# Remainders of the weights on GpSimd instead of VectorE, in a two-layer hybrid trunk

## The chip, the cores and the metric

The kernel runs on one core of a Trainium2 chip. The time is what the device takes for one execution, in microseconds. TensorE is called PE below (PEld its weight loads), VectorE DVE, ScalarE ACT, GpSimd POOL, and SyncE SP; these are the names in the profile.

## The reference, cut to what matters

Two layers over 512 tokens of width 1024, float32. Layer 0 mixes by attention: 8 heads of forgetting attention (softmax with a cumulative decay) and 8 stick-breaking heads, head size 64. Layer 1 mixes by a gated short convolution. Each mixer is followed by a gated MLP of width 2816 with a causal convolution of width 3.

```python
h = x
for layer in range(DEPTH):
    i = layer // 2
    if layer % 2 == 0:
        h = h + attention_mixer(h, ...)      # proj = rms_norm(h) @ w_in ; 16 heads ; o @ w_out
    else:
        h = h + short_conv_mixer(h, ...)     # gate_b * conv3(gate_c * u) @ w_out
    h = h + conv_ffn(h, ...)                 # u = conv3(rms_norm(h) @ w_up); (silu(g) * val) @ w_down
```

## The kernel before, in words

Every product with a weight matrix is made of three passes of PE in a reduced format, so that the result keeps nearly float32's precision: a number a is written as hi + lo, where hi is a rounded to the format (float32r) and lo is the remainder a - hi; the product is hi x hi + hi x lo + lo x hi (`mm3`, and `mm3_rhs` where the weights are the moving operand). The activations are split in this way where they arise; the weights are split when they are loaded.

**The weights' pipeline.** The program writes down all 198 pieces of weights in the order of their use (`want`); a piece ("chunk") is up to 128 x 1056 numbers, mostly 128 x 1024. `weights()` hands out the next chunk and before that calls `load` for as many as keep two in advance. For one chunk, `load` issues the DMA into `raw` (by SP, L223), then the main copy `whi` on ACT (L226), then, through `rest`, the remainder `wlo` = raw - whi (L233). `raw`, `whi` and `wlo` have three buffers each: a new main copy waits until PE has done its last matmul with the main copy of three chunks ago, and the DMA of a chunk waits until the remainder of three chunks before has read its buffer.

**The stages.** First come the transposes of x and the first norm. Then attention, up to about 310 us: the projections run as `columns`, tokens on the partitions ("token-major"), two chunks for each of queries (L490 to L492, kind 0), keys and values of four groups of four heads. `heads` takes the sums of squares (L521, L523), the reciprocal root (`rsqrt`, ten small DVE steps, L316 to L328) and scales (L532, L535); `turn_heads` transposes and splits (L549 to L554). `logits` makes the scores of a pair of heads for half of the tokens (L571 to L577); for forgetting heads softmax follows (L588 to L595), for stick-breaking ones two sigmoids, a scan (L604) and a product (L605). `turn` transposes the weights of attention (L623) and splits them into `pt` (L625, L628); POOL fills a part of each `pt` with zeros (L633). `weigh` multiplies by the values (L647, L648) and adds up (L657, L658); `output` applies the output projection to a group (L248 to L250). The projections of later groups are generators that are run in small bits between these steps (`fill`). After that come the MLP's up-projection (44 chunks), its down-projection (24), the short convolution, and the second MLP, whose down-projection runs with the weights as the moving operand again.

The order in the program is an order of wishes: a scheduler that works with its own estimates of each instruction's cost puts the final order on every engine, and each engine then works strictly in that order.

Of the kernel before, what the change touches and what calls it, by code (L numbers as in the profile page):

```python
# [22 lines left out]
ALU = mybir.AluOpType  # L23
# [25 lines left out]
def trunk(  # L49
# [7 lines left out]
    act, dve, pe, pool = nc.scalar, nc.vector, nc.tensor, nc.gpsimd  # L57
# [13 lines left out]
    def f32(ap):  # L71
        return ap.bitcast(F32)
# [89 lines left out]
    def behind(later, earlier):  # L162

        tc.add_manual_dep(
            later.ins, earlier.ins.name,
            mybir.DependencyInfo(mybir.DependencyClass.NoSync, mybir.DependencyReason.DATA), reason="order",
        )
# [11 lines left out]
    def after(us, fn):  # L179
        later.append((clock[0] + us, len(later), fn))  # L180
        later.sort(key=lambda e: e[0])
# [31 lines left out]
    def load(i, last=None):  # L213
        dram, k0, nk, parts = wanted[i]
        n = sum(parts[1::2])
        raw = wp.tile([P, CHUNK], F32, tag="raw", name=f"raw{i}")
        hi = wp.tile([P, CHUNK], F32R, tag="whi", name=f"whi{i}", bufs=3)
        lo = wp.tile([P, CHUNK], F32R, tag="wlo", name=f"wlo{i}", bufs=3)
        v = raw[:, 0:nk * n].rearrange("p (k c) -> p k c", c=n)
        to = 0  # L220
        for c0, width in zip(parts[::2], parts[1::2]):
            with nc.allow_non_contiguous_dma(reason="eight columns"):
                nc.sync.dma_start(  # L223
                    v[:, :, to:to + width], dram[k0 * P:(k0 + nk) * P, c0:c0 + width].rearrange("(k p) c -> p k c", p=P))
            to += width
        made = act.activation(hi[:, 0:nk * n], raw[:, 0:nk * n], AF.Copy)  # L226
        if last is not None:
            behind(made, last)

        def rest():  # L230
            if i in unsplit:
                unsplit.remove(i)
                dve.tensor_tensor(lo[:, 0:nk * n], raw[:, 0:nk * n], f32(hi[:, 0:nk * n]), op=ALU.subtract)  # L233
        unsplit.add(i)
        after(LATER, rest)
        return rest, [t[:, 0:nk * n].rearrange("p (k c) -> p k c", c=n) for t in (hi, lo)]
# [682 lines left out]
```

## Time and profile before

| | us |
|---|---|
| median of 3 runs | 1243.5 (1242.23 to 1245.99) |
| the profiled execution | 1243.43, of which span 1241.7 |
| busy in the span: PE, DVE | 1207.4, 765.5 |
| busy in the span: ACT, POOL | 500.3, 21.2 |

A row of the timeline reads: start, duration (us), engine, line, operation, tile written <- tiles read, shape, count, and in brackets how long the engine had stood idle before it and who released it. Tile names stand without their buffer numbers. Rows on waits read: engine, line, who released it, microseconds in total, times, longest.

### The profile page before, as it was taken

To read this page: it belongs to the slowest core of one execution; us is meant where nothing else is said; L and a number is where in the kernel's file an instruction comes from. 1 tells how busy PE (TensorE), PEld (TensorE's weight loads), DVE (VectorE), ACT (ScalarE), POOL (GpSimd) and SP (SyncE) were. 2 spreads that over 40 slices of the span, in tenths; PEclk is the share of its full clock that TensorE was granted. 3 is DMA by queue.
4 is the path that set the end of the run, shared out by engine and by line. 5 is a ranking of instruction groups with operands and counts; after the bars stand their busy time and mean duration, and the time that the engine had idled before them with its cause. 6 is when DMAs were issued, how large, how long until landed. Compare 5 with 4: busy or idle time off the path is not lost.

```text
span 1241.7 us, 15526 instructions
## 1 busy us (share of the span) xinstructions
PE 1207.4 (97%) x6129; PEld 1002.8 (81%) x6129; DVE 765.5 (62%) x1248; ACT 500.3 (40%) x814; POOL 21.2 (2%) x101
## 2 busy tenths in 40 slices
PE   8999999898999999999999999999999999999998
PEld 7988988776888888888888888888888888888886
DVE  6687778787767777773333555555777676762212
ACT  6465665555444434342222222233444344442120
POOL 3000000000000000000000000000000000000000
PEclk9999999999999999999999999999999999999999
DMA  5312212111233333323333333333233323232330
GB/s 175 104 45 59 57 46 69 34 52 51 86 102 89 98 97 90 102 81 93 94 94 98 102 87 100 89 98 100 88 94 93 102 86 102 87 100 85 109 112 34
DMA packets 175273, 108.16 MB, mean 87 GB/s; under 512 B 4604, under 2 KB 168492, under 8 KB 175200
## 3 DMA queue, kind: packets, MB, share of 16 engines
q1 hardware_dynamic: 174944, 107.01, 29.0%
q8 instruction: 48, 0.79, 0.3%
q0 software_dynamic: 256, 0.16, 0.1%
q14 instruction: 25, 0.20, 0.1%
HBM read 105.06 MB, written 2.10 MB: 86 GB/s over the span
## 4 chain that ended last, share of the span: by engine, by line
PE 88%; DVE 7%; ACT 3%; issue 1%; DMA 1%; SPq 0%; DVEq 0%; ACTq 0%
PE psb L248 11%; PE psb L250 11%; PE psb L249 11%; PE psa L248 11%; PE psa L249 11%; PE psa L250 11%; PE psa L490 4%; PE psa L492 4%; PE psa L491 4%; PE psb L492 2%; PE psb L491 2%; PE psb L490 2%; DVE rest L604 1%; PE psc L623 1%; ACT whi L226 1%; DVE wlo L233 1%
## 5 line engine op out<-in xcount | busy, mean ns | idle before, releaser
L226 ACT ACTIVATE whi<-raw 128x1024 fp32r<-128x1024 f32 (+2 forms) x198 | 208.3, 1053 | 360.2 <-PE psb L249 130.9
L233 DVE TENSOR_TENSOR wlo<-raw,whi 128x1024 fp32r<-128x1024 f32 (+2 forms) x198 | 240.3, 1214 | 169.5 <-ACT whi L226 168.6
L248 PE MATMUL psb<-hs_hi,whi 128*128 128x512 f32 x480 | 189.9, 396 | 0.0
L250 PE MATMUL psb<-hs_hi,wlo 128*128 128x512 f32 x480 | 189.9, 396 | 0.0
L249 PE MATMUL psb<-hs_lo,whi 128*128 128x512 f32 x480 | 188.8, 393 | 0.0
L248 PE MATMUL psa<-hs_hi,whi 128*128 128x512 f32 x416 | 164.7, 396 | 0.0
L250 PE MATMUL psa<-hs_hi,wlo 128*128 128x512 f32 x416 | 164.3, 395 | 0.0
L249 PE MATMUL psa<-hs_lo,whi 128*128 128x512 f32 x416 | 164.0, 394 | 0.0
L340 DVE SCALAR_TENSOR_TENSOR u<-y,taps,u 128x510 f32<-128x510 f32 (+1 forms) x176 | 130.9, 747 | 3.0
L490 PE MATMUL psa<-whi,hs_hi 128*128 128x256 f32 (+1 forms) x352 | 102.7, 293 | 10.7 <-DVE v L484 7.7
L249 PEld LDWEIGHTS psb<-hs_lo,whi 128*128 128x128 f32 x480 | 90.1, 188 | 21.5
L250 PEld LDWEIGHTS psb<-hs_hi,wlo 128*128 128x128 f32 x480 | 90.1, 188 | 21.4
L248 PEld LDWEIGHTS psb<-hs_hi,whi 128*128 128x128 f32 x480 | 90.3, 188 | 20.3
L491 PE MATMUL psa<-wlo,hs_hi 128*128 128x256 f32 (+1 forms) x352 | 100.6, 286 | 0.4 <-DVE wlo L233 0.4
L492 PE MATMUL psa<-whi,hs_lo 128*128 128x256 f32 (+1 forms) x352 | 100.9, 287 | 0.0
L250 PEld LDWEIGHTS psa<-hs_hi,wlo 128*128 128x128 f32 x416 | 78.1, 188 | 18.7
L249 PEld LDWEIGHTS psa<-hs_lo,whi 128*128 128x128 f32 x416 | 78.1, 188 | 18.4
L248 PEld LDWEIGHTS psa<-hs_hi,whi 128*128 128x128 f32 x416 | 78.2, 188 | 18.0
L793 DVE TENSOR_TENSOR y<-psb,nrow_n 128x512 f32<-128x512 f32 x44 | 30.4, 691 | 83.9 <-PE psb L250 83.9
L490 PEld LDWEIGHTS psa<-whi,hs_hi 128*128 128x128 f32 x352 | 67.4, 192 | 13.1 <-DVE v L484 8.6
L332 ACT ACTIVATE a<-u 128x512 fp32r<-128x512 f32 x44 | 27.8, 633 | 118.6 <-DVE u L798 118.6
L491 PEld LDWEIGHTS psa<-wlo,hs_hi 128*128 128x128 f32 x352 | 67.6, 192 | 0.6 <-DVE wlo L233 0.6
(225 smaller groups left out, 1939.8 us busy)
## 6 DMA issues: line engine op xcount, KB each, us to landing
raw<-in_ffn_w_up SPq DMA_DIRECT2D x88, 512.0 KB, 3.8
raw<-in_ffn_w_down SPq DMA_DIRECT2D x30, 512.0 KB, 3.7
raw<-in_attn_w_in SPq DMA_DIRECT2D x24, 512.0 KB, 3.9
raw<-in_conv_w_in SPq DMA_DIRECT2D x24, 512.0 KB, 3.8
raw<-in_ffn_w_down SPq DMA_DIRECT2D x16, 448.0 KB, 3.7
raw<-in_attn_w_out SPq DMA_DIRECT2D x8, 512.0 KB, 4.0
raw<-in_conv_w_out SPq DMA_DIRECT2D x8, 512.0 KB, 3.9
x_tok<-in_x SPq DMA_DIRECT2D x4, 512.0 KB, 7.7
```

The costliest lines, as they stand in the source:

```text
L226: made = act.activation(hi[:, 0:nk * n], raw[:, 0:nk * n], AF.Copy)
L233: dve.tensor_tensor(lo[:, 0:nk * n], raw[:, 0:nk * n], f32(hi[:, 0:nk * n]), op=ALU.subtract)
L248: pe.matmul(acc, w[0], rhs[0], start=first, stop=False)
L249: pe.matmul(acc, w[0], rhs[1], start=False, stop=False)
L250: pe.matmul(acc, w[1], rhs[0], start=False, stop=last)
L332: act.activation(hi, src, AF.Copy)
L340: dve.scalar_tensor_tensor(dst[:, d:], src[:, 0:S - d], tap(j), dst[:, d:], op0=ALU.mult, op1=ALU.add)
L490: pe.matmul(acc, lhs[0], w[0], start=first, stop=False)
L491: pe.matmul(acc, lhs[0], w[1], start=False, stop=False)
L492: pe.matmul(acc, lhs[1], w[0], start=False, stop=last)
L604: dve.tensor_tensor_scan(back, back, back, 1.0, op0=ALU.mult, op1=ALU.bypass)
L793: dve.tensor_tensor(y, acc, norm.row, op=ALU.mult)
```

## The change

One word in `load`: the remainder is computed on POOL, not on DVE. What is computed stays the same.

```diff
@@ def rest():
             if i in unsplit:
                 unsplit.remove(i)
-                dve.tensor_tensor(lo[:, 0:nk * n], raw[:, 0:nk * n], f32(hi[:, 0:nk * n]), op=ALU.subtract)
+                pool.tensor_tensor(lo[:, 0:nk * n], raw[:, 0:nk * n], f32(hi[:, 0:nk * n]), op=ALU.subtract)
```

The scheduler moves other instructions with it. On DVE, at the last keys of group 3, where a pair of remainders and the scans of the first stick-breaking heads meet (- before, + now):

```order
-L233 TENSOR_TENSOR wlo_3103<-raw_3101,whi_3102 128x1024
 L523 TENSOR_REDUCE qv_2853<-sq_3070 128x8
 L526 TENSOR_TENSOR qv_2853<-qv_2853,rx_115 128x16
-L233 TENSOR_TENSOR wlo_3108<-raw_3106,whi_3107 128x1024
 L527 TENSOR_SCALAR qv_2853<-qv_2853 128x16
-L604 SCALAR_TENSOR_TENSOR rest_3164<-rest_3164 128x383
 L316 TENSOR_SCALAR rh_qk_3138<-qv_2853 128x16
 L318 TENSOR_SCALAR rs_qk_3140<-qv_2853 128x16
+L320 TENSOR_SCALAR rg_qk_3142<-rs_qk_3140 128x16
+L324 TENSOR_TENSOR ra_qk_3144<-rg_qk_3142 128x16
+L326 TENSOR_TENSOR rb_qk_3146<-ra_qk_3144,rh_qk_3138 128x16
+L328 SCALAR_TENSOR_TENSOR ry_qk_3148<-rb_qk_3146,rg_qk_3142 128x16
```

Both remainders are gone from DVE's queue, and the steps of `rsqrt` now stand before the first scan instead of between the scans.

On POOL, in the part of the queue for forgetting heads, the fills of `pt` stood alone before:

```order
L633 MEMSET pt_1933 128x128
L633 MEMSET pt_1934 128x128
L633 MEMSET pt_1935 128x128
L633 MEMSET pt_1936 128x128
L633 MEMSET pt_2157 128x128
```

Now a pair of remainders stands among them, each with the DMA and ACT's main copy to wait for:

```order
L633 MEMSET pt_1935 128x128 [waits DVE_49,PE_49]
L633 MEMSET pt_1936 128x128 [waits PE_49]
L233 TENSOR_TENSOR wlo_1996<-raw_1994,whi_1995 128x1024 [waits DMAHW2_49,Activation_49]
L233 TENSOR_TENSOR wlo_2001<-raw_1999,whi_2000 128x1024 [waits DMAHW3_49,PE_49,Activation_49]
L633 MEMSET pt_2157 128x128 [waits DVE_49,PE_49,Pool_49]
```

All 198 remainders are on POOL in this way. On PE, at the start, in the first queries (chunks 170 and 229, accumulators of token blocks 0, 1 and 2 being psa_240, psa_371 and psb_399):

```order
+L490 MATMUL psb_399<-whi_170,hs_hi 128x256
+L491 MATMUL psb_399<-wlo_171,hs_hi 128x256
+L492 MATMUL psb_399<-whi_170,hs_lo 128x256
 L490 MATMUL psa_240<-whi_229,hs_hi 128x256
 L490 MATMUL psa_371<-whi_229,hs_hi 128x256
+L490 MATMUL psb_399<-whi_170,hs_hi 128x256
+L491 MATMUL psb_399<-wlo_171,hs_hi 128x256
+L492 MATMUL psb_399<-whi_170,hs_lo 128x256
```

Matmuls of the third token block with the first chunk have moved ahead of the first use of the second chunk's remainder.

## The prediction

> **What bounds the kernel now.** I read the page's busy times first, then the busy time of two stretches, then what TensorE (PE) waited for, then the chain that ended last.
>
> ```profile
> span 1241.7 us, 15526 instructions
> PE 1207.4 (97%) x6129; PEld 1002.8 (81%) x6129; DVE 765.5 (62%) x1248; ACT 500.3 (40%) x814; POOL 21.2 (2%) x101
> L226 ACT ACTIVATE whi<-raw 128x1024 fp32r<-128x1024 f32 (+2 forms) x198 | 208.3, 1053 | 360.2 <-PE psb L249 130.9
> L233 DVE TENSOR_TENSOR wlo<-raw,whi 128x1024 fp32r<-128x1024 f32 (+2 forms) x198 | 240.3, 1214 | 169.5 <-ACT whi L226 168.6
> ```
> ```profile
> 31.00:310.00 279.00, 254.58 (x1909) 228.84 (x1908) 215.43 (x521) 157.00 (x371) 11.69 (x62) 0.98 0.20 58
> 310.00:1242.00 932.00, 927.55 (x4025) 749.77 (x4023) 530.77 (x683) 322.50 (x406) 0.00 (x0) 1.00 0.31 93
> ```
>
> The columns of the last two rows are PE, weight load, VectorE (DVE), ScalarE (ACT), GpSimd (POOL). From 310 us on PE is busy 927.55 of 932 us: nothing that DVE sheds can shorten that stretch, it can only be lengthened. The attention stretch before it has 24 us in which PE stands still, with DVE busy 215.43 of 279 us. What PE waited for there (us, times, longest):
>
> ```profile
> PE psa L490 <- DVE v L484: 7.7, 3, 4.9
> PE psc L623 <- DVE pt L628: 4.2, 4, 2.6
> PE psa L248 <- DVE o L658: 2.6, 2, 2.0
> PE psa L490 <- DVE o L658: 1.8, 2, 1.1
> PE psc L549 <- DVE qk L535: 1.7, 2, 1.5
> ```
> ```profile
> by line: PE psa L490 9.2%; PE psa L492 8.5%; PE psa L491 8.4%; DVE rest L604 6.0%; PE psc L623 4.6%; DVE wlo L233 4.3%; PE psa L248 4.2%; ACT whi L226 3.8%; PE psa L249 3.7%; PE psb L571 3.6%; PE psa L250 3.6%; issue 3.2%; DVE w L605 3.0%;
> ```
>
> These five rows come to 18.0 us, all released by DVE. In the chain of that stretch the remainders themselves (DVE wlo L233) hold 4.3%, 12.0 of 279 us. So DVE's queue sets the end here, and the change is decided in this stretch and at the few places where a remainder is used as soon as it is made.
>
> **The price of one remainder on POOL.** The trace has no large two-input instruction on POOL, so I bound it by fills.
>
> ```profile
> L438 POOL MEMSET fwide<- 128x512 f32 x1 | 0.5, 546 | 0.0
> L633 POOL MEMSET pt<- 128x128 f32 x64 | 12.1, 216 | 258.7 <-PE psa L647 195.0 <-DVE fboth L454 48.4 <-DVE top L588 14.4
> ```
>
> From 128 to 512 elements a fill grows by 330 ns, 0.86 ns an element. A pass over 1024 elements is then 0.99 us, two passes 1.87, three (two reads, one write, one after another) 2.75. It can't be less than one pass, and I know of no row that makes it more than three. I take 2.3 us, midway between two and three, against 1.21 on DVE. The Trainium skill, GPSIMD Engine Reference, section Performance versus the Vector engine, gives 4497 ns for 2048 elements of such an addition; an estimate of half of it is 2.25 us, and the sum below would be 0.35 us less; no run shows it yet. In total 198 x 2.3 = 455 us, 37% of the span, so POOL itself bounds nothing.
>
> **Remainders that come late.** The main copy (whi) is made when PE lets go of its buffer; the remainder follows at once, and PE uses it at a fixed distance. Where that distance is under 2.3 us, PE waits for the difference.
>
> ```profile
> 16.38 1.22 DVE L233 TENSOR_TENSOR wlo<-raw,whi 128x1024 fp32r<-128x1024 f32 x1 [0.19 <-ACT whi L226]
> 17.66 0.38 PE L491 MATMUL psa<-wlo,hs_hi 128*128 128x256 f32 x1 [0.40 <-DVE wlo L233]
> 12.64 2.09 POOL L113 DMA_DIRECT2D spare<-in_ffn_conv x4
> ...
> 26.77 1.23 DVE L233 TENSOR_TENSOR wlo<-raw,whi 128x1024 fp32r<-128x1024 f32 x1 [0.54 <-ACT whi L226]
> 28.30 0.28 PE L490 MATMUL psa<-whi,hs_hi 128*128 128x256 f32 x1
> 28.42 0.28 PE L491 MATMUL psa<-wlo,hs_hi 128*128 128x256 f32 x1
> ...
> 193.08 1.22 DVE L233 TENSOR_TENSOR wlo<-raw,whi 128x1024 fp32r<-128x1024 f32 x1 [0.49 <-ACT whi L226]
> 194.73 0.28 PE L491 MATMUL psa<-wlo,hs_hi 128*128 128x256 f32 x1
> ```
> ```profile
> 675.45 1.23 DVE L233 TENSOR_TENSOR wlo<-raw,whi 128x1024 fp32r<-128x1024 f32 x1 [3.40 <-ACT whi L226]
> 684.57 0.39 PE L250 MATMUL psb<-hs_hi,wlo 128*128 128x512 f32 x1
> 1158.53 1.23 DVE L233 TENSOR_TENSOR wlo<-raw,whi 128x1024 fp32r<-128x1024 f32 x1 [4.37 <-ACT whi L226]
> 1160.27 0.40 PE L491 MATMUL psa<-wlo,a 128*128 128x512 f32 x1
> 1221.88 1.23 DVE L233 TENSOR_TENSOR wlo<-raw,whi 128x1024 fp32r<-128x1024 f32 x1 [4.37 <-ACT whi L226]
> 1223.62 0.40 PE L491 MATMUL psa<-wlo,a 128*128 128x512 f32 x1
> ```
>
> - The start (16.38): 1.28 us from start to use, with 0.40 of waiting already. It would be 1.0 us later, but the new order puts nine matmuls of the third token block before that use, at 0.12 us each (28.30 to 28.42) about 1.05 us: nothing. POOL's small DMA issues, now behind the first remainder, end 1.1 us after their old 14.73, still before 16.38.
> - Four places in attention (first 26.77, last 193.08): 1.65 us to the use. 4 x 0.65 = 2.6; two matmuls moved ahead at the first take 0.2 off: **+2.4 us**.
> - Three places in the last projection (first 1158.53, last 1221.88): 1.74 us. 3 x 0.56 = **+1.7 us**. Nothing else is ready for PE there, and the last one lies 20 us before the end.
> - Elsewhere from 310 us on the smallest distance is 9.1 us (675.45 to 684.57): hidden by two chunks of lead, several times over. If POOL were held up to 9 us there, the cover would be gone and every chunk would pay.
>
> Sum +4.1 us; with 0.99 us a remainder 0, with 2.75 us +7.2.
>
> The load of the chunk three further on waits for the remainder to have read its buffer, so it starts some 1.1 us later; its main copy waits longer for PE to let go of whi, so that costs nothing while the lead of 9.1 us stands.
>
> The pt fills on POOL (L633), which wait for PE, now stand among the remainders; in the trace those put ahead of a remainder ran before its main copy was done, and a fill is used a unit later, so I cost the mixing at nothing; if a fill came late, each remainder behind it would be late by as much.
>
> **What DVE gains or loses in attention.** One place, the largest stall, shows it:
>
> ```profile
> 210.37 1.23 DVE L233 TENSOR_TENSOR wlo<-raw,whi 128x1024 fp32r<-128x1024 f32 x1 [3.15 <-ACT whi L226]
> 211.51 0.68 DVE L523 TENSOR_REDUCE qv<-sq 128x8 f32<-128x512 f32 x1
> 212.22 0.17 DVE L526 TENSOR_TENSOR qv<-qv,rx 128x16 f32<-128x16 f32 x1
> 212.33 1.23 DVE L233 TENSOR_TENSOR wlo<-raw,whi 128x1024 fp32r<-128x1024 f32 x1
> 213.55 0.95 DVE L604 TENSOR_TENSOR_SCAN rest<-rest 128x383 f32<-128x383 f32 x1
> 222.10 0.41 PE L490 MATMUL psa<-whi,hs_hi 128*128 128x256 f32 x1 [4.93 <-DVE v L484]
> 222.83 0.69 DVE L535 TENSOR_TENSOR qk<-qk,qr 128x512 f32<-128x512 f32 x1
> ```
> ```profile
> 222.00:226.00 4.00, 3.90 (x20) 3.91 (x21) 2.36 (x7) 0.42 (x1) 0.00 (x0) 0.57 0.00 0
> ```
>
> Lower end: DVE is simply relieved, PE gets all of the chain's 12.0 us, and the half clock behind this stall (granted 0.57 for 4 us, 1.7 us lost) goes too: -13.7. Upper end: DVE's instructions with two inputs in SBUF (L526, the scans L604, L535, the rsqrt steps) can't read while POOL reads its two. Remainders come in pairs 1.96 us apart at six places (here 210.37 and 212.33); on POOL a pair takes 4.6 us from the first start, where DVE was through after 3.19: +1.4 each, 8.4. Two single ones (the first at 236.09) add 2.3 - 1.2 = 1.1 each: +10.6. The rows don't show two such readers at once; the nearest is a fill beside a remainder, and that only writes:
>
> ```profile
> 235.93 0.83 POOL L633 MEMSET pt<- 128x128 f32 x4 [18.82 <-PE psa L647]
> 236.09 1.22 DVE L233 TENSOR_TENSOR wlo<-raw,whi 128x1024 fp32r<-128x1024 f32 x1
> ```
>
> DVE's 1.22 us are the usual length there, so writing doesn't disturb. The Trainium skill, SBUF — State Buffer, section Who interferes with whom, says that a DVE instruction with two SBUF inputs and a GpSimd one that reads SBUF exclude each other for the whole instruction, while one that only writes does not; by that rule in full the result would be 1258.1. The trace agrees with the second half; no run shows the first. It speaks against this change.
>
> I take **+6**: most rows of the example behind the remainder read two tiles, but L523 and those reading PSUM don't. The new DVE order speaks against much relief as well: the rsqrt chain, ten small steps each needing the one before, now stands undivided ahead of the first scan L604.
>
> **Sum**, on the profiled execution of 1243.43 us (span 1241.7 and 1.7 around it; the median of the runs is 1243.5): +4.1 + 6 = +10.1, so **1253.5 us**.
>
> **Rivals.**
> - *DVE is relieved* (faster). Mechanism: POOL's reading doesn't hold DVE, and the two remainders ahead of v L484 and o L658 are gone. For: 18.0 us of PE waits are DVE's. Against: the order just named, and ACT's copies stand on the same path. Three quarters of 12.0, the 1.7 of clock, and the late remainders: -9.0 - 1.7 + 4.1 = -6.6, 1236.9 us. It decides as soon as DVE's rows beside POOL keep their lengths.
> - *Hidden*: DVE is relieved but ACT or PE's order is late next, and only late remainders count: +4.1, 1247.5 us; with one pass on POOL 1243.4.
>
> That the change isn't done is no rival: the new order has all 198 on POOL.
>
> **How the numbers follow.** Forecast case 0.5 (1247 to 1261), relieved 0.3 (1230 to 1243), hidden 0.2 (1243 to 1248). Range 1235 to 1261: the top is +7.2 + 10.6 (1261.3), the bottom leaves out the better third of the relieved case. 0.3% is 3.7 us, about what a measurement of this kernel can tell. Faster 0.26 (the relieved case but for its weak end), same 0.11 (0.04 of that, and a third of hidden, 0.07), slower 0.63.
>
> **What would show it.** Right: remainders of about 2.3 us on POOL; DVE's L526, L604 and L535 beside them stretched well over 0.17, 0.95 and 0.69 us; PE waits named POOL wlo at seven places, half a microsecond each; 310 to 1158 us unchanged. Wrong: DVE's rows of the old length and the 4.93 us stall cut to under 3; or remainders of 5 us and more, so that PE waits for POOL in the up-projection, which would take the time past the range.

## The result, and the profile after

| | before | after |
|---|---|---|
| median of 4 runs each, same chip (us) | 1244.74 (1242.23 to 1246.97) | 1307.38 (1298.95 to 1312.18) |
| ratio, 95% interval | | 1.0497 (1.0432 to 1.0561) |
| the profiled execution (us), span | 1243.43, 1241.7 | 1310.73, 1309.0 |

The change costs 63 us, five per cent. Slower was forecast, but the time came out 54 us above the forecast, and the range ended at 1261. The page of the changed kernel, the rows that answer to those of before, and for the taps of the up-projection (L340) the row of before as well:

```profile
span 1309.0 us, 15630 instructions
PE 1238.3 (95%) x6129; PEld 1020.9 (78%) x6129; DVE 746.4 (57%) x1050; ACT 494.4 (38%) x814; POOL 496.3 (38%) x299
L233 POOL TENSOR_TENSOR wlo<-raw,whi 128x1024 fp32r<-128x1024 f32 (+2 forms) x198 | 476.0, 2407 | 713.8 <-ACT whi L226 695.4
L340 DVE SCALAR_TENSOR_TENSOR u<-y,taps,u 128x510 f32<-128x510 f32 (+1 forms) x176 | 250.3, 1425 | 109.3 <-ACT u L337 106.3
```
```profile
L340 DVE SCALAR_TENSOR_TENSOR u<-y,taps,u 128x510 f32<-128x510 f32 (+1 forms) x176 | 130.9, 747 | 3.0
```

240 us of remainders left DVE, and DVE's busy time fell by 19 (765.5 to 746.4). The taps alone took 119 back: 1425 ns for an instruction that took 747, with nothing changed in it. What PE waits for in the whole program:

```profile
PE psc L549 <- DVE qk L535: 18.8, 4, 7.7
PE psc L623 <- DVE pt L628: 9.6, 5, 2.6
PE psa L491 <- POOL wlo L233: 5.3, 8, 0.9
PE psa L248 <- DVE v L484: 5.0, 1, 5.0
PE psa L490 <- DVE o L658: 4.9, 2, 2.5
PE psb L250 <- POOL wlo L233: 4.7, 15, 1.0
...
PE psa L490 <- DVE y L793: 2.6, 1, 2.6
```

POOL itself is named for 10.0 us. The long waits are DVE's, as they were before, but for other tiles. The stages by the first or last matmul of each, in the profiled executions (us; the columns on the right belong to experiments below):

| stage | before | after | POOL, old order | DVE, new order | POOL in pieces | POOL from MLP | the same, y in PSUM |
|---|---|---|---|---|---|---|---|
| start to the first scores | 61.1 | 66.1 | 66.7 | 62.1 | 63.7 | 61.5 | 61.8 |
| attention to the last output product | 253.2 | 296.8 | 279.7 | 269.5 | 267.9 | 257.4 | 254.5 |
| up-projection, layer 0 | 247.3 | 253.1 | 251.4 | 247.3 | 247.5 | 253.3 | 249.0 |
| down-projection, layer 0 | 122.3 | 123.8 | 123.8 | 122.3 | 122.3 | 123.9 | 122.3 |
| short convolution | 179.9 | 180.2 | 180.1 | 179.9 | 180.0 | 180.1 | 180.1 |
| up-projection, layer 1 | 246.9 | 250.7 | 250.1 | 246.9 | 247.1 | 250.6 | 247.3 |
| last projection | 131.0 | 138.2 | 136.7 | 130.9 | 132.4 | 138.3 | 133.6 |

The 67.3 us of the two spans are +5.0 at the start, +43.6 in attention and +18.7 behind it. At the start PE is idle 2.9 us longer, most of it for the first scaled heads (L549 waits 3.0 us for qk L535, 0.2 before), and its own work takes 2.1 us longer. Single executions differ by about 4 us in attention: the two right-hand kernels have the same work there as before, on DVE, and show 257.4 and 254.5 against 253.2.

**Who holds DVE.** The timeline of the changed kernel at the last keys of group 3, DVE and POOL:

```profile
243.73 4.75 POOL L233 TENSOR_TENSOR wlo<-raw,whi 128x1024 fp32r<-128x1024 f32 x2 [14.17 <-ACT whi L226]
244.69 0.69 DVE L523 TENSOR_REDUCE qv<-sq 128x8 f32<-128x512 f32 x1 [5.26 <-ACT sq L521]
245.41 0.74 DVE L526 TENSOR_TENSOR qv<-qv,rx 128x16 f32<-128x16 f32 x1
246.19 2.33 DVE L527 TENSOR_SCALAR qv<-qv 128x16 f32<-128x16 f32 x1
248.55 0.17 DVE L316 TENSOR_SCALAR rh_qk<-qv 128x16 f32<-128x16 f32 x1
```

L526 and L527 work on sixteen numbers a partition. L526 ends with POOL's first remainder, L527 with its second, at 248.5; as soon as POOL is through, the next step takes 0.17 us. The reduction L523, which ran beside the first remainder, kept its 0.69. The 176 taps of the up-projections show it in numbers: in this trace 86 of them began while a remainder ran on POOL, and each of these ended 0.54 to 0.55 us behind POOL's end; the 90 others took 736 to 752 ns.

**What a stall costs beyond itself.** The same place a little later, PE's timeline, then the busy time of two stretches (PE, weight load, DVE, ACT, POOL, then the granted clock):

```profile
258.41 1.51 PE L549 MATMUL psc<-ident,qk 128*128 128x128 f32 x6 [7.70 <-DVE qk L535]
```
```profile
252.00:256.00 4.00, 0.00 (x0) 0.00 (x0) 3.96 (x9) 2.44 (x6) 0.00 (x0) 0.71 0.00 0
256.00:262.00 6.00, 3.59 (x17) 3.62 (x18) 4.88 (x10) 1.95 (x4) 0.00 (x0) 0.50 0.00 0
```

The clock falls to half during the wait, and PE goes on at half clock for some microseconds behind it. The same 1687 PE instructions of attention, in before, in the kernel with POOL in the old order, and in the changed kernel; then in the control of an experiment below, whose attention is that of before:

```profile
61.10:314.30 253.20, 229.90 (x1687) 204.19 (x1687) 199.02 (x469) 145.57 (x351) 11.69 (x62) 0.97 0.18 53
```
```profile
66.70:346.40 279.70, 239.43 (x1687) 211.71 (x1687) 203.61 (x443) 144.88 (x349) 70.79 (x87) 0.93 0.16 46
```
```profile
66.10:362.90 296.80, 250.93 (x1688) 221.91 (x1687) 203.50 (x443) 145.07 (x349) 70.53 (x87) 0.88 0.15 43
```
```profile
62.70:320.30 257.60, 235.84 (x1687) 209.55 (x1687) 198.93 (x469) 145.45 (x351) 11.71 (x62) 0.94 0.18 52
```

From before to the changed kernel PE stands idle 22.6 us longer (23.3 to 45.9), and its work takes 21.0 us longer (229.9 to 250.9) at a clock of 0.88 in place of 0.97. By these two executions half of attention's loss is the clock. That half is less sure than the waiting: the control has the long waits of before and less idle time (21.8 us), yet its PE needs 235.8 us at 0.94. Measured from there, 15.1 us are the slower clock. DVE's busy time for the same work rose by 4.5 us: all that the remainders freed there was given back, and a little more.

### The profile page after: what moved, and what is told of

It is laid out like the page before. It is cut to its first block, busy times and chain, and to the rows that moved or that the text cites. A ratio compares the mean times of both kernels' runs of the same rounds, so it can differ in the third digit from the quotient of the medians.

```text
span 1309.0 us, 15630 instructions
## 1 busy us (share of the span) xinstructions
PE 1238.3 (95%) x6129; PEld 1020.9 (78%) x6129; DVE 746.4 (57%) x1050; ACT 494.4 (38%) x814; POOL 496.3 (38%) x299
## 4 chain that ended last, share of the span: by engine, by line
PE 47%; issue 25%; POOL 16%; DVE 8%; ACT 2%; DMA 1%; POOLq 0%; SPq 0%; DVEq 0%; ACTq 0%
POOL wlo L233 16%; PE psb L248 6%; PE psb L250 6%; PE psb L249 6%; PE psa L248 6%; PE psa L250 6%; PE psa L249 6%; PE psa L490 2%; PE psa L491 2%; PE psa L492 2%; DVE rest L604 2%; PE psc L623 1%; DVE qv L527 1%; DVE w L605 1%; PE psb L571 1%
## 5 line engine op out<-in xcount | busy, mean ns | idle before, releaser
L233 POOL TENSOR_TENSOR wlo<-raw,whi 128x1024 fp32r<-128x1024 f32 (+2 forms) x198 | 476.0, 2407 | 713.8 <-ACT whi L226 695.4
L340 DVE SCALAR_TENSOR_TENSOR u<-y,taps,u 128x510 f32<-128x510 f32 (+1 forms) x176 | 250.3, 1425 | 109.3 <-ACT u L337 106.3
L248 PE MATMUL psb<-hs_hi,whi 128*128 128x512 f32 x480 | 189.8, 395 | 0.0
L248 PE MATMUL psa<-hs_hi,whi 128*128 128x512 f32 x416 | 164.7, 396 | 0.7 <-DVE h L779 0.7
L490 PE MATMUL psa<-whi,hs_hi 128*128 128x256 f32 (+1 forms) x352 | 106.5, 303 | 7.6 <-DVE o L658 4.9
L491 PE MATMUL psa<-wlo,hs_hi 128*128 128x256 f32 (+1 forms) x352 | 104.9, 298 | 3.4 <-POOL wlo L233 3.4
L248 PEld LDWEIGHTS psb<-hs_hi,whi 128*128 128x128 f32 x480 | 90.3, 188 | 19.5
L248 PEld LDWEIGHTS psa<-hs_hi,whi 128*128 128x128 f32 x416 | 78.2, 188 | 18.2 <-issue 1.1
L332 ACT ACTIVATE a<-u 128x512 fp32r<-128x512 f32 x44 | 27.9, 633 | 167.0 <-DVE u L798 167.0
L490 PEld LDWEIGHTS psa<-whi,hs_hi 128*128 128x128 f32 x352 | 71.1, 202 | 9.7 <-issue 5.4
L491 PEld LDWEIGHTS psa<-wlo,hs_hi 128*128 128x128 f32 x352 | 71.2, 202 | 4.4 <-POOL wlo L233 4.4
L797 ACT ACTIVATE u<-u 128x512 f32<-128x512 f32 x44 | 27.8, 633 | 120.2 <-DVE u L340 120.2
```

The source lines that it names most:

```text
L233: pool.tensor_tensor(lo[:, 0:nk * n], raw[:, 0:nk * n], f32(hi[:, 0:nk * n]), op=ALU.subtract)
L248: pe.matmul(acc, w[0], rhs[0], start=first, stop=False)
L332: act.activation(hi, src, AF.Copy)
L340: dve.scalar_tensor_tensor(dst[:, d:], src[:, 0:S - d], tap(j), dst[:, d:], op0=ALU.mult, op1=ALU.add)
L490: pe.matmul(acc, lhs[0], w[0], start=first, stop=False)
L491: pe.matmul(acc, lhs[0], w[1], start=False, stop=False)
```

## The experiments

The theory from these traces: while POOL reads its two tiles, DVE's instructions with inputs in SBUF stand still (the lock); in attention the new order of PE adds to it. The rival: the remainders are simply late, and the rest follows from PE's waiting for them.

**POOL's remainders in the old order.** The instructions that both kernels have are put into one of the two orders by a list, without any wait. The list stands ahead of the program, so all lines of this kernel's rows are 86 higher.

```diff
+        for x, y in zip(seq, seq[1:]):
+            tc.add_manual_dep(
+                y, x.name, mybir.DependencyInfo(mybir.DependencyClass.NoSync, mybir.DependencyReason.DATA), reason="order")
...
+    pin((mybir.EngineType.PE, PE_ORDER))
+    pin((mybir.EngineType.Activation, ACTIVATION_ORDER))
+    pin((mybir.EngineType.DVE, DVE_ORDER))
```

> Remainders on POOL as in the change, but every other instruction of PE, ACT and DVE is issued in the order of the kernel before (a written list). Theory 'lock and order' (POOL's remainder holds DVE's SBUF instructions off, and the new order of PE puts the head transposes L549 ahead of work that could cover DVE): the up- and down-projections keep their +19 us, attention gives back most of its +48, so 1265 to 1280 us. Theory 'lock alone' (order does not matter): 1295 to 1310. Theory 'late remainders alone' (PE waits for wlo, order and lock do not matter): 1300 to 1310, as the remainders are no earlier.

Measured: 1290.49 us, ratio 1.0365 (1.0339 to 1.0392). That is outside the ranges of all three theories, between the two for the lock: the old order gives back 17.1 us of attention's 43.6, not most of it. What PE waited for (L576 and L334 are L490 and L248 of before, L577 and L319 are L491 and L233, L570 is L484, L709 and L714 are L623 and L628, L635 and L621 are L549 and L535):

```profile
PE psa L576 <- DVE v L570: 14.2, 3, 6.5
PE psa L577 <- POOL wlo L319: 5.7, 8, 1.1
PE psc L709 <- DVE pt L714: 5.4, 4, 2.6
...
PE psa L334 <- DVE v L570: 4.3, 1, 4.3
PE psc L635 <- DVE qk L621: 4.2, 2, 3.0
```

The largest wait is the one of before (v L484), nearly doubled from 7.7 us. As both kernels have the same 6129 PE instructions in the same order, the start of each can be compared. The delay is 4.8 us at 46 us of the kernel before, 7.7 at 98, 18.5 at 177, 29.6 at 253, 33.8 at 319. It never falls by more than 1 us from the highest value it had. So in this order there is no stretch of attention where a remainder on POOL brings PE forward by much.

**DVE's remainders in the new order.** The same list, but the other way round: remainders on DVE, everything else as in the changed kernel. Lines are 82 higher.

> Remainders on DVE as before, but every other instruction of PE, ACT and DVE is issued in the order of the changed kernel (a written list; the remainders find their own places in DVE's queue). Theory 'lock and order': the new order costs something by itself even without POOL, since PE meets the transposes L549 before DVE has their scaled heads: 1252 to 1275 us. Theory 'lock alone': 1241 to 1249. Theory 'late remainders alone': 1241 to 1249.

Measured: 1261.02 us, ratio 1.0127 (1.0096 to 1.0158), within the range for lock and order; attention 269.5 us, 16.3 more than before, and nothing behind it. Waits of PE in attention (L631 and L617 are L549 and L535, L705 and L710 are L623 and L628, L330 and L566 are L248 and L484):

```profile
PE psc L631 <- DVE qk L617: 12.0, 4, 6.1
PE psc L705 <- DVE pt L710: 7.3, 5, 2.6
...
PE psa L330 <- DVE v L566: 1.7, 1, 1.7
```

All of DVE's groups have the lengths of before here. The order is a cost of its own, and the two add up: 253.2 + 26.5 + 16.3 = 296.0, against the 296.8 of the changed kernel. With about 4 us between single executions, so close a fit is partly luck. Where the order differs on PE, at the place of the 7.70 us wait (- before, + now; psc_3205 and psc_3214 are the transposed heads, psa_3271 an accumulator of the projection):

```order
 L492 MATMUL psa_3112<-whi_3102,hs_lo 128x256
+L549 MATMUL psc_3205<-ident,qk_2851 128x128 x2
+L549 MATMUL psc_3214<-ident,qk_2597 128x128 x2
...
 L490 MATMUL psa_3271<-whi_2861,hs_hi 128x256
 L491 MATMUL psa_3271<-wlo_2862,hs_hi 128x256
-L549 MATMUL psc_3205<-ident,qk_2851 128x128 x2
-L549 MATMUL psc_3214<-ident,qk_2597 128x128 x2
```

The transposes that need DVE's scaled heads now stand ahead of matmuls of the projection. Those matmuls had a wait for DVE of their own at this place: 4.93 us before, for v L484. With DVE's remainders in the new order the transposes wait 6.1 us here, so the new wait takes the place of an old one and only the difference counts. Over attention PE is idle 7.4 us longer than before (23.3 to 30.7); the rest of the 16.3 us is slower work (229.9 to 238.9 us), of which the control above shows 5.9 without any change in attention.

**PE's new order alone.** PE's list of the changed kernel, with remainders on DVE; DVE and ACT are left to the scheduler.

> Remainders on DVE as before, and only PE's instructions are issued in the order of the changed kernel (a written list); DVE and ACT are ordered freely by the scheduler. Theory 'the new order of PE costs by itself' (it meets head transposes L549 before DVE has scaled the heads): 1253 to 1264 us, as with all three orders, and PE's waits for L535 stay near 12 us. Rival 'it is the new order of DVE or ACT': 1242 to 1250, waits for L535 near 2 us.

Measured: 1259.47 us, ratio 1.0104 (1.008 to 1.0128).

```profile
PE psc L549 <- DVE qk L535: 13.6, 4, 6.3
PE psc L623 <- DVE pt L628: 10.0, 7, 2.6
```

So PE's order is enough to cost as much as all three orders. The stages differ a little: +12.7 us in attention and +3.7 at the start (1.0 at the start with all three). Which of its moves costs how much isn't shown.

**A second reader on POOL.** The kernel before in its own order; behind DVE's remainder POOL subtracts the same two tiles once more, into raw, which is dead by then.

```diff
                 dve.tensor_tensor(lo[:, 0:nk * n], raw[:, 0:nk * n], f32(hi[:, 0:nk * n]), op=ALU.subtract)
+                pool.tensor_tensor(raw[:, 0:nk * n], raw[:, 0:nk * n], f32(hi[:, 0:nk * n]), op=ALU.subtract)
```

> The kernel before in its own order, with a second subtraction of the same two tiles on POOL for each chunk behind DVE's; its result goes into raw, which is not needed any more, so nothing waits for it but the next load of that buffer. PE, ACT and DVE have nothing more to do. Theory 'lock' (DVE's SBUF instructions stand still while POOL reads): DVE's busy time grows by over 100 us, the small instructions such as L527 up to 2.3 us, and the time is 1265 to 1310 us. Theory 'late remainders alone': 1243 to 1250, since the remainders are as early as before.

**A second writer on POOL.** The same with two fills of raw in its place.

> As the kernel with the second subtraction on POOL, but POOL makes two fills of the same raw tile (about 2 us together, no reads) in its place. Theory 'lock by POOL's reads': no instruction of DVE gets longer, 1242 to 1248 us. Rival 'any work of POOL in SBUF slows DVE': nearly as slow as with the subtraction, 1260 to 1300. Rival 'the later release of raw is what costs': the same time as with the subtraction, with DVE's instructions at their old length.

Measured: 1412.22 us with the subtraction, ratio 1.1344 (1.1314 to 1.1374), and 1258.53 with the fills, ratio 1.0107 (1.0078 to 1.0136). Groups of the first (lines 121 higher: L461 is L340), with PE's two largest waits in total, then of the second (122 higher: L462 is L340, L438 is the step L316 of `rsqrt`):

```profile
L354 POOL TENSOR_TENSOR raw<-raw,whi 128x1024 f32<-128x1024 f32 (+2 forms) x198 | 529.5, 2675 | 758.1 <-DVE wlo L353 706.6 <-issue 18.3 <-ACT w L711 13.3
L461 DVE SCALAR_TENSOR_TENSOR u<-y,taps,u 128x510 f32<-128x510 f32 (+1 forms) x176 | 304.7, 1734 | 3.0
```
```profile
PE psb L371 <- DVE wlo L353: 26.7, 35, 0.8
PE psa L371 <- DVE wlo L353: 18.5, 35, 0.7
```
```profile
L354 POOL MEMSET raw<- 128x1024 f32 (+2 forms) x198 | 187.6, 948 | 750.1 <-DVE wlo L353 724.3 <-ACT w L712 12.0 <-issue 7.0
L462 DVE SCALAR_TENSOR_TENSOR u<-y,taps,u 128x510 f32<-128x510 f32 (+1 forms) x176 | 131.0, 747 | 3.0
L438 DVE TENSOR_SCALAR rh_qk<-qv 128x16 f32<-128x16 f32 x8 | 6.4, 798 | 0.2
```

With the reader, DVE's busy time goes from 765.5 to 1046.0 us though DVE has nothing more to do, and each up-projection takes 292 to 294 us in place of 247. Nobody uses what POOL makes here, so a late result of POOL can't be the cause, and the rival, which gave 1243 to 1250, falls. A later release of raw isn't the cause either: the fills delay it too, by two times 0.95 us against 2.68. Lateness is still a way by which the hold reaches PE: the remainders that PE uses are made on DVE, which is held, and PE waits 45.2 us for them, nearly all in the up-projections. The cost was far above the expected one, presumably because DVE has the remainders still to make here and is held as well. With the writer the taps keep their 747 ns to the nanosecond. But the fills are not free, and the time lies in none of the three ranges: the one-input steps of `rsqrt` (L316, L318, L320) take 0.7 to 0.8 us instead of 0.17, and attention takes 266.6 us instead of 253.2, of which about 4 can be the execution. The Trainium skill, SBUF — State Buffer, section Who interferes with whom, has both rules: two inputs in SBUF contend with POOL's reads only, while `tensor_scalar` can run in a mode that takes the shared pair and is then blocked by any POOL instruction that holds it. The trace agrees with both (747 against 1734 ns; 0.8 against 0.17 us), though it doesn't show the mode.

**One tile read by POOL.** POOL multiplies raw by 0.5 in place.

> As the kernel with the second subtraction on POOL in the old order, but POOL multiplies the raw tile by 0.5 in place: one tile read instead of two (the result is not used). Theory 'any read of SBUF by POOL locks': DVE's taps L340 are held off as before for as long as this instruction lasts, DVE's busy time grows by over 100 us. Rival 'the lock takes two operands of POOL in SBUF': the taps stay at 0.75 us, and only one-input instructions such as L316 get longer, as with the fills; 1250 to 1262 us.

Measured, in two runs: 1267.73 us, ratio 1.0169 (1.0134 to 1.0204).

```profile
L233 POOL TENSOR_SCALAR raw<-raw 128x1024 f32<-128x1024 f32 (+2 forms) x198 | 592.5, 2994 | 558.6 <-DVE wlo L233 519.5 <-DVE w L595 11.7 <-issue 8.2
L340 DVE SCALAR_TENSOR_TENSOR u<-y,taps,u 128x510 f32<-128x510 f32 (+1 forms) x176 | 187.6, 1069 | 3.0
```
```profile
507.78 2.19 DVE L340 SCALAR_TENSOR_TENSOR u<-y,taps,u 128x511 f32<-128x511 f32 x2
508.01 3.16 POOL L233 TENSOR_SCALAR raw<-raw 128x1024 f32<-128x1024 f32 x1 [2.02 <-DVE wlo L233]
510.00 0.69 DVE L798 TENSOR_TENSOR u<-u,u 128x512 f32<-128x512 f32 x1
```

One read is enough to hold DVE's two-input instructions: the rival with two operands falls. But the other theory's "as long as this instruction lasts" falls as well. DVE's busy time grew by 90 us (855.5), under the 100 expected and a third of what the subtraction cost, though POOL's instruction lasted longer. The rows show when the hold ends: the second tap is through at 509.97, and the product L798, which reads two tiles too, takes its usual 0.69 us, while POOL's instruction goes on to 511.17. All taps that began in the first 0.7 us of such an instruction ended 1.0 to 1.2 us ahead of its end, where those beside a subtraction ended 0.55 us behind it. Whether this instruction reads in its first part only, or its end in the profile is late (spans on POOL are rough there), stays open.

**From the MLP on.** Remainders on DVE for the 32 chunks of attention, on POOL for the other 166.

```diff
-                dve.tensor_tensor(lo[:, 0:nk * n], raw[:, 0:nk * n], f32(hi[:, 0:nk * n]), op=ALU.subtract)
+                (dve if i < 32 else pool).tensor_tensor(lo[:, 0:nk * n], raw[:, 0:nk * n], f32(hi[:, 0:nk * n]), op=ALU.subtract)
```

> The 32 chunks of attention (indices 0 to 31) keep their remainders on DVE, the 166 later ones have them on POOL. PE's order is that of the kernel before throughout. Theory 'lock': each up-projection gets 3 to 6 us longer, the last projection 6 to 7, the rest 2, attention nothing: 1256 to 1264 us. Rival 'the damage after attention is only carried over from attention' : 1243 to 1249 us.

**The same, with one operand of the taps in PSUM.**

```diff
-                y = work.tile([P, S], F32, tag="y", name=f"y{layer}{j}{half}")
+                y = bank("c")
```

> As the kernel with POOL's remainders from the MLP on, but the tile y of the up-projections (L793) lies in PSUM, in the two banks 'c' that stand empty there, so that the taps L340 read one operand from PSUM and one from SBUF. Theory 'only DVE instructions with both inputs in SBUF are held off by POOL's reads': the 176 taps stay under 0.8 us, the main copies are no longer late, and both up-projections come back to 247 us; the time is 3 to 8 us below that kernel's. Rival 'POOL's remainder is late by itself in the up-projections' (the lock of L340 does not matter): the same time as that kernel within 2 us, PE still waits about fifteen times for wlo. Rival 'any DVE instruction that touches SBUF is held off': L340 stays at over 1.2 us mean.

> The kernel before with y in PSUM in the up-projections and nothing else changed: the control for the kernel with both. All theories: within 2 us of the kernel before, since PE bounds that stage; L340 between 0.6 and 0.9 us.

Measured: 1266.34 us from the MLP on, ratio 1.0159 (1.0129 to 1.0188); 1251.65 with y in PSUM, 1.0053 (1.0035 to 1.0071); the control 1247.94, 1.0007 (0.9989 to 1.0024). The first is 2 us above what was expected, of which attention, unchanged, shows 4. So the damage behind attention is made there. The second lies 14.7 us below the first, where 3 to 8 were expected: the up-projections gave back 7.6 us in the profiled executions, the last projection 4.7, the down-projection 1.6, and attention, alike in both, 2.9. How the damage is made, in the changed kernel's timeline of a pair of chunks of the up-projection:

```profile
566.75 2.41 POOL L233 TENSOR_TENSOR wlo<-raw,whi 128x1024 fp32r<-128x1024 f32 x1 [3.09 <-ACT whi L226]
567.31 3.17 DVE L340 SCALAR_TENSOR_TENSOR u<-y,taps,u 128x511 f32<-128x511 f32 x2 [1.72 <-ACT u L337]
571.25 0.64 ACT L332 ACTIVATE a<-u 128x512 fp32r<-128x512 f32 x1 [3.97 <-DVE u L798]
571.78 1.04 ACT L226 ACTIVATE whi<-raw 128x1024 fp32r<-128x1024 f32 x1
572.90 2.40 POOL L233 TENSOR_TENSOR wlo<-raw,whi 128x1024 fp32r<-128x1024 f32 x1 [3.75 <-ACT whi L226]
575.36 0.50 PE L250 MATMUL psb<-hs_hi,wlo 128*128 128x512 f32 x1 [0.31 <-POOL wlo L233]
```

It is a ring: POOL's remainder holds the taps (3.17 us for two, 1.5 without), ACT waits with its next instruction for the product behind the taps (3.97 us; all 44 such waits come to 167.0 us, 118.6 before), the next main copy stands behind that in ACT's queue, the next remainder behind the main copy, and PE meets it 0.31 us too early. Fourteen such waits, 3.7 us together, lie in the two up-projections; the fifteenth, 0.98 us, is in the down-projection. The up-projections got 9.6 us longer: PE is idle 5.3 us there, and its matmuls take 4.3 us longer at full clock, for which no row gives the reason. With y in PSUM, remainders still on POOL at the same length:

```profile
L233 POOL TENSOR_TENSOR wlo<-raw,whi 128x1024 fp32r<-128x1024 f32 (+1 forms) x166 | 400.2, 2411 | 543.8 <-ACT whi L226 543.8
L340 DVE SCALAR_TENSOR_TENSOR u<-psc,taps,u 128x510 f32<-128x510 f32 (+1 forms) x176 | 131.4, 749 | 68.7 <-ACT u L337 65.8
```
```profile
PE psa L491 <- POOL wlo L233: 1.9, 3, 0.6
```

The taps are back at 749 ns, though 173 of the 176 began beside a remainder. The waits in the up- and down-projections are gone: behind attention PE waits three times in the last projection (the last row) and twice, 0.55 and 0.62 us, where the MLP begins. Both up-projections return to 249.0 and 247.3 us. The Trainium skill says in the same section that a DVE instruction with at most one SBUF input, outside the modes just named, doesn't contend with GpSimd; this run agrees.

**In pieces.** POOL's remainders in the old order of the rest, four subtractions of 256 columns to a chunk.

> As the kernel with POOL's remainders in the order of the kernel before (a written list), but each remainder is made in pieces of 256 columns, four to a chunk. Theory 'lock by whole instructions': an instruction of DVE waits for at most one piece, about 0.7 us, so no small instruction such as L527 lasts over 1.0 us (2.8 there), attention gives back 5 to 15 of its 27 us, and the time is 1272 to 1287 us. Rival 'POOL's share of SBUF's bandwidth is what slows DVE': DVE's sums stay as they were and the time is 1288 to 1300, the pieces' fixed cost added. Rival 'late remainders': each chunk is later by three fixed costs, 1292 to 1310.

Measured: 1263.24 us, ratio 1.0142 (1.0116 to 1.0168), better than the lock theory's own range: attention gives back 11.8 us, as that theory had it, but the stages behind it give back 12.7 and the start 3.0, which it left out.

```profile
L233 POOL TENSOR_TENSOR wlo<-raw,whi 128x256 fp32r<-128x256 f32 (+1 forms) x794 | 692.0, 902 | 469.8 <-ACT whi L226 455.9 <-PE psb L577 7.1 <-DVE pt L628 6.7
L527 DVE TENSOR_SCALAR qv<-qv 128x16 f32<-128x16 f32 x8 | 4.9, 613 | 0.2
```

POOL needs 3.6 us for a chunk in place of 2.4, and the kernel is 27 us faster than with whole ones in the same order. DVE is held for less at one time (L527 0.61 us against 1.91 with whole ones). This run alone doesn't show that the hold is all of it: PE also starts on the first piece before the last is made (a first use at 17.74 us, 0.80 after POOL began the chunk), and its waits for wlo fall from 8.9 us in 18 places to 1.4 in 3. The kernel stays slower than the one before.

## Why the prediction was wrong, step by step

The step that failed is the term for DVE in attention: the hold was named and near in size, but it was carried to the end of the kernel one for one. Two more terms were put at nothing: PE's new order, and all that lies between 310 us and the last projection.

- *The price of a remainder on POOL*: 2.3 us taken, 2407 ns measured. Right, as is that POOL itself bounds nothing (38% against 37%).
- *Late remainders*: seven places were named. In the last projection the three waits came, 1.9 us in all where 1.7 was put. In attention all four came (0.51, 0.69, 0.67 and 0.95 us), 2.8 us where 2.4 was put. At the start the wait of 0.40 us became 0.55, where nothing was put. In all that is +4.9 us against +4.1: the mechanism was right and the size near.
- *"Elsewhere from 310 us on ... hidden by two chunks of lead"* failed: +11.4 us in the two up-projections, the down-projection and the convolution, though only 4.7 us of it are waits for wlo. The distance of 9.1 us was read from before, where the main copies came in time. The lock was priced in attention alone; what it does where PE doesn't wait for DVE wasn't asked, and there it came back through ACT's queue. The mechanism that the text gave for such a loss, POOL held up by 9 us, wasn't needed.
- *Up to the first scores* 5.0 us were lost. Late remainders are 1.4 of that, as two of the four places lie there. The wait of L549 for L535 grew by 2.8 and PE was 2.1 us slower, both put at nothing; other waits fell by 1.3.
- *The last projection* was put at +1.7 and measured +7.2. The rest is its entrance: DVE, late with the last taps, hands over y 2.6 us after PE could have used the bank, and PE goes on at half clock (3.4 us of it).
- *DVE in attention, +6 in a range of -13.7 to +10.6*, is the step that failed most. As DVE's own time it came near: DVE's busy time grew by 4.5 us. That is partly luck, as the instructions held were not those of the list. The error was to carry that time to the end one for one. The places where it falls are steps of chains for which PE waits, the wait is followed by half clock, and the prediction counted the clock only as a gain (1.7 us). With the order held, 4.6 us of DVE (199.0 to 203.6) became 17.0 us of idle PE (23.3 to 40.3) and 9.5 us of slower PE: 26.5. The waiting is the sure part; measured from the control, whose PE needs 235.8 us, only 3.6 us of the slower PE are left. The upper end, +10.6, was no bound either way.
- *Which instructions are held*: L526 as said, L604 in three of its 32 executions. L535 wasn't met by a remainder at all (0.69 us still), nor were most `rsqrt` steps, which are twelve and not ten. The worst, L527, has one input; it wasn't on the list.
- *The order*: the prediction read what the scheduler moved on DVE and, on PE, at the start. PE's new order in attention, with L549 ahead of the projections, was not priced: +16.3 us in one execution, 12.7 with PE's order alone.
- *The rivals*: "DVE is relieved" and "hidden" are both refuted. What was named as proof against the forecast, remainders of 5 us, didn't occur; PE came to wait for POOL in the up-projection all the same.

## What to carry to other kernels

Before moving a two-input operation from DVE to GpSimd, list what DVE runs at the same time with its inputs in SBUF, in every stage, also those where DVE isn't the bound: of the 240 us taken off DVE, 221 came back as time in which its other instructions were held. What helps is an operand of DVE's in PSUM (taps back from 1425 to 749 ns) or short pieces on GpSimd (27 us back); here neither brought the kernel below its time before. A scheduler's new order is a change of its own: hold the order of the rest by a list and measure the two apart.

## What the runs showed of the hardware

- Beside a subtraction on POOL, a DVE instruction with two SBUF inputs is held to POOL's end: 86 of 176 taps ended 0.54 to 0.55 us behind it, the others took 0.75 us.
- Fills on POOL, which read nothing, lengthen one-input DVE steps on sixteen numbers from 0.17 to 0.8 us, and leave two-input instructions at 747 ns to the nanosecond.
- A POOL instruction with one read held DVE's taps to 1069 ns on average, with two reads to 1734, though the first lasted longer (2994 against 2675 ns): beside the one read, taps that began in its first 0.7 us were through 1.0 to 1.2 us before its end.
- A long wait of PE is paid twice: the granted clock was 0.50 from 256 to 262 us, around the end of a wait of 7.7 us, and in attention the slower clock cost 15 to 21 us beside 23 to 24 us of waiting, by the execution it is measured from. What the clock costs varies: the same attention work with the same long waits took PE 229.9 and 235.8 us in two executions.
